# One layer of a hybrid diffusion backbone on one core: a third buffer for low parts, an own buffer for the vector product's tiles, its sums by a column of ones, and context decays made in place and earlier

## The chip, the cores and the metric

The kernel runs on one core of one Trainium2 chip. The time is the device time of one execution in microseconds (us), the median of the runs shown. The profile comes from one further execution. Its engines are named as the profile names them: PE (TensorE: matmuls; PEld is its weight load), DVE (VectorE), ACT (ScalarE), POOL (GpSimd) and SP (SyncE, which here only issues DMA transfers, in order).

## The reference

The layer has 256 latent tokens and 256 context tokens of width 2048, all in float32. Cut to what matters here:

```python
mod  = silu(c) @ w_mod + b_mod            # 6 x 2048 shifts, scales, gates; the same for the context
h    = modulate(rms_norm(x), sh1, sc1);   hc = the same for the context
q, ff, fb, v, g, a, b = split(h @ w_in)   # eight heads of 128 keys and 128 values
# per head and direction (forward with ff, backward with fb): f = lb + (1-lb)*sigmoid(ff)
#   S_t = diag(f_t) S_{t-1} + (1-f_t) v_t^T ;  o_t = S_t^T silu(q_t)
#   the latent scan starts from the final state of the context scan
y    = concat(readout(o_f + o_b, g), silu(group_norm(dwconv31(a * sigmoid(b))))) @ w_out
x    = x + g1 * rms_norm(y)
h2   = modulate(rms_norm(x), sh2, sc2)
x    = x + g2 * rms_norm((gelu(dwconv3x3(h2 @ up_gate)) * (h2 @ up_val)) @ ffn_down)
```

## The kernel before, in words

**Matmuls.** Every weight is split into a high part (`whi`, rounded to the type that PE reads at full rate) and a low part (`wlo`, the rest), and so is every activation. A product is three matmuls: high by high, high by low, low by high (`mm3_w`, `mm3_x`, lines 192 to 210). A weight tile is 128 x 2048 values, 1 MB. `wtile` (line 130) brings one: SP issues its DMA into a `raw` buffer (line 127), ACT casts it to `whi` (line 137), DVE subtracts to `wlo` (line 140). `take` hands out a tile and stages the one after it.

**Buffers.** `raw` has three buffers, `whi` three, `wlo` two. The three `raw` buffers are shared: the tiles of the modulation weights for the vector product (`graw`, line 702) use them as well. A buffer comes free when DVE has made the low part (line 140), or has added the last half of a `graw` tile (line 713).

**The vector product.** Four of the six modulation vectors (numbers s = 2 to 5) are not made on PE. For each s, 16 tiles arrive one after the other, and DVE multiplies each by its 128 values of silu(c), one per partition, and adds it to `gacc` (128 x 2048), in two halves per tile (line 713). `GEMV_H`, `GEMV_G` and `GEMV_W` say after which matrix product how many of these tiles are handed out. In the first phases their priority is lowered by `gemv_prio` = -1000. Then `gacc` has to be summed over the 128 partitions, with the result laid out as columns (`mod_cols`, line 718): in four visits PE transposes four blocks each, and ACT copies each block with an accumulated sum.

**Stages.** Phase 0 (to 158.9 us) makes the first modulation vectors, the hidden input `hT`, and v. Its tiles `mraw` are put in turn into eight free buffers of `raw`, `whi` and `wlo`. Then come eight heads: per head the products ff, fb, q (`head_gemm`), then b and a (`conv_gemm`); then eight products g. Phase 2 is the output projection and the first residual, phase 3 the wide layer up (gate and val), phase 4 the layer down.

**The attention of a head** (`head`, line 775) is spawned when its q is made, and runs under the products of the head after it. DVE and ACT first make the decays, keys and queries of seven levels in turn (lines 799 to 826, the "level chain": each level's scaling on DVE reads what ACT and DVE left of the level before). After 22 us of counted matmul time (`Y_DG`) PE comes by for the scores (line 837, tiles `lv` and `cr`). Then the diagonal blocks are picked by masks on DVE (line 850) and copied by ACT. Two scans on DVE make the context decays (lines 868 and 870) into two of the four rows of `att`, and the context keys are multiplied by them (line 873). After a further 6.5 us PE comes by for the context scores (`cx`, line 878), then for `o` (line 886), then for its transpose.

**What sets the order.** From the heads on, PE's order is the written program's (`self.order({ET.PE})`): the visits stand at fixed places between the products, and PE waits where an operand is late. DVE, ACT and SP are ordered ahead of time by a planner that goes by priority and its own durations; weight tiles are moved ahead by 600, `graw` sums put back by 1000. On the chip every engine then keeps that order, so an instruction whose operand is late holds back all that stand behind it.

Of the kernel before, what the change touches and what calls it, by code (L numbers as in the profile page):

```python
# [8 lines left out]
F32 = mybir.dt.float32  # L9
# [6 lines left out]
P = 128  # L16
# [19 lines left out]
ACT_M = 64  # L36
GEMV_H = {"ff": 2, "fb": 0, "q": 1, "b": 1, "a": 0}
GEMV_G = 0.2
# [20 lines left out]
    ("lnb", HEADS),  # L59
    ("hgw", 1),  # L60
    ("fcw", NFF * 9),
    ("fcb", NFF),
]
_POFF = {}
_n = 0
for _name, _w in _PCOLS:
    _POFF[_name] = (_n, _n + _w)
    _n += _w
NPAR = _n

# [43 lines left out]
class _Kernel:  # L114
# [15 lines left out]
    def wtile(self, i, prio=600, hi=None, lo=None):  # L130

        src, (oh, ol) = self.srcs[i], self.places[i]
        raw = self.raws.pop(0) if self.raws else self.raw_tile(src, prio)
        with self.tc.high_priority(prio):
            if hi is None:
                hi = self.stg.tile([P, WBUF], F32R, tag="whi", name="whi", bufs=3)[:, oh:oh + 2048]
            self.nc.scalar.copy(hi, raw)  # L137
            if lo is None:
                lo = self.stg.tile([P, WBUF], F32R, tag="wlo", name="wlo", bufs=2)[:, ol:ol + 2048]
            self.nc.vector.tensor_sub(lo, raw, hi.bitcast(F32))  # L140
        return hi, lo
# [81 lines left out]
    def par(self, name, i=0, n=1):  # L223
        o = _POFF[name][0]
        return self.params[:, o + i:o + i + n]

# [14 lines left out]
    def run(self):  # L241
# [44 lines left out]
        self.pax = px  # L286
        self.gemv_prio = -1000
        self.order(P0_ENG)
# [44 lines left out]
        self.hid_lo = hid.tile([P, NFF, SEQ], F32R, name="hid_lo")  # L333
        upp, up = enter(name="up", bufs=2, side="right")
        self.phase3(up)
        leave(upp)
# [12 lines left out]
    def consts(self):  # L349
# [47 lines left out]
        self.ab = cst.tile([P, 2, KB, 2], F32, name="ab")  # L397
        self.mc = cst.tile([P, 4, KB], F32, name="mc")

    def late_consts(self):  # L400
# [10 lines left out]
    def phase0(self, p0, px, srcs):  # L411
# [49 lines left out]
        def gemv_row(q, t):  # L461

            if t == 0:
                rows[q] = px.tile([P, 512], F32, tag="row", name="row", bufs=P0_ROW)
            tag, n = (("raw", 3), ("whi", 3), ("wlo", 2), ("raw", 3), ("whi", 3), ("wlo", 2), ("raw", 3), ("whi", 3))[self.nt % 8]
            self.nt += 1
            w = self.stg.tile([P, 2048 if tag == "raw" else WBUF], F32, tag=tag, name="mraw", bufs=n)[:, 0:2048]
            nc.sync.dma_start(w, a["wm1"][q, t])
# [306 lines left out]
    def head(self, h, st):  # L775
# [23 lines left out]
        for m in LEVELS:  # L799
# [16 lines left out]
            else:  # L816
                ts = T[:, :, toff:toff + nb]
                for i, o in enumerate(range(0, SEQ, 2 * m)):
                    e0, e1 = slice(o, o + m), slice(o + m, o + 2 * m)
                    for t, d, e, f in ((Q, 0, e0, ts[:, 0, 2 * i + 1:2 * i + 2]), (Q, 1, e1, ts[:, 1, 2 * i:2 * i + 1]),  # L820
# [37 lines left out]
        for j in range(4):  # L858
            r = slice(32 * j, 32 * (j + 1))
            nc.scalar.copy(_ap(att[r], 32 * j, [[SEQ + P, 2], [1, 32]]), diag[r])  # L860
# [7 lines left out]
        nc.vector.tensor_tensor_scan(_ap(E, SEQ - 2, [[-1, n]]), _ap(FF, 512 + 512 - 1, [[-1, n]]),  # L868
                                     _ap(FF, 512 + 512 - 1, [[-1, n]]), 1.0, op0=ALU.mult, op1=ALU.bypass)
        nc.vector.tensor_tensor_scan(E[:, 1, 1:SEQ], FF[:, 0, SEQ:SEQ + n], FF[:, 0, SEQ:SEQ + n], 1.0,  # L870
                                     op0=ALU.mult, op1=ALU.bypass)
        kc = KK[:, :, SEQ:512]
        nc.vector.tensor_mul(kc, kc, E)
        yield Y_CX
# [355 lines left out]
def _pack(inputs):  # L1230
# [27 lines left out]
    }  # L1258
    a["params"] = np.ascontiguousarray(np.concatenate([parts[n] for n, _ in _PCOLS], axis=1))
    i = np.arange(P)  # L1260
# [18 lines left out]
```

## Time and profile before

| | |
|---|---|
| three runs | 1419.16, 1422.34, 1422.53 us; median 1422.34 |
| profiled execution, its own time | 1419.87 us |
| its span, first to last instruction | 1418.1 us |
| mean granted PE clock | 0.995 |
| PE busy | 97% of the span |
| DVE busy | 76% |
| ACT busy | 51% |
| DMA queue of SP | 62.7% of 16 engines |

Busy times of matmuls are modelled and overlap each other, so a stage with PE at 100% has matmuls in an unbroken row; an idle time shown ahead of a matmul is a lower bound of what was lost there. "idle before <- X" names who ended a wait. Times inside the span count from its first instruction.

### The profile page before, as it was taken

The numbers are of one execution on the slowest core, as the hardware profiler recorded it, in microseconds if no ns is written. First come the engines' busy times: TensorE is split into PE (matmuls) and PEld (weight loads), VectorE is DVE, ScalarE is ACT, GpSimd is POOL, SyncE is SP. The second block draws the span as 40 slices with busy tenths as digits, with TensorE's granted clock in tenths as the row PEclk, the third lists the DMA queues.
The fourth block names the chain that finished last, engine by engine and source line by source line (L and its number), as shares of the span: only waits on it lengthen the run. The fifth ranks groups of instructions, "written<-read, shape, count | busy, mean of one in ns | idle before, by whom it ended". The sixth has DMA issues, their size and how long they took to land.

```text
span 1418.1 us, 24793 instructions
## 1 busy us (share of the span) xinstructions
PE 1375.5 (97%) x10272; PEld 1224.9 (86%) x10272; DVE 1073.3 (76%) x1577; ACT 716.6 (51%) x1174; POOL 31.2 (2%) x57
## 2 busy tenths in 40 slices
PE   4999999999999999999999999999999999999997
PEld 2566888888888898988999999999999998888886
DVE  4444788999999899777788788778878886767544
ACT  4333456666656665536744444454545443333532
POOL 0000001001000011000000000000000000000000
PEclk9999999999999999999999999999999999999999
DMA  9988676446645565788355555555555558878652
GB/s 374 391 325 330 258 267 218 160 188 238 222 167 207 208 226 189 286 305 302 123 205 180 205 185 203 181 206 189 199 184 203 193 194 340 312 287 306 242 187 106
DMA packets 49153, 329.38 MB, mean 232 GB/s; under 512 B 5392, under 2 KB 5648, under 8 KB 10896
## 3 DMA queue, kind: packets, MB, share of 16 engines
q1 hardware_dynamic: 49040, 327.80, 62.7%
q8 instruction: 80, 1.31, 0.4%
q14 instruction: 33, 0.27, 0.1%
HBM read 323.58 MB, written 4.19 MB: 231 GB/s over the span
## 4 chain that ended last, share of the span: by engine, by line
PE 77%; DVE 11%; ACT 4%; DMA 3%; issue 2%; POOL 2%; SPq 0%; DVEq 0%; POOLq 0%; ACTq 0%
PE val L197 6%; PE val L199 6%; PE val L198 6%; PE dn L206 6%; PE gate L197 6%; PE dn L208 6%; PE gate L199 5%; PE dn L207 5%; PE gate L198 5%; DVE wlo L140 3%; DVE acc L930 3%; PE v L206 2%; PE wo L208 2%; PE wo L206 2%; PE wo L207 2%
## 5 line engine op out<-in xcount | busy, mean ns | idle before, releaser
L137 ACT CAST whi<-raw 128x2048 fp32r<-128x2048 f32 x193 | 368.9, 1912 | 371.3 <-PE val L198 120.1
L140 DVE TENSOR_TENSOR wlo<-raw,whi 128x2048 fp32r<-128x2048 f32 x193 | 441.9, 2289 | 149.4 <-PE dn L207 59.7
L199 PE MATMUL val<-h,wlo 128*128 128x256 f32 x704 | 194.3, 276 | 0.0
L197 PE MATMUL val<-h,whi 128*128 128x256 f32 x704 | 194.3, 276 | 0.0
L198 PE MATMUL val<-h,whi 128*128 128x256 f32 x704 | 194.3, 276 | 0.0
L197 PE MATMUL gate<-h,whi 128*128 128x256 f32 x688 | 189.9, 276 | 0.0
L198 PE MATMUL gate<-h,whi 128*128 128x256 f32 x688 | 189.9, 276 | 0.0
L199 PE MATMUL gate<-h,wlo 128*128 128x256 f32 x688 | 189.9, 276 | 0.0
L1139 DVE SCALAR_TENSOR_TENSOR gacc<-gate,params,gacc 128x189 f32<-128x189 f32 (+2 forms) x352 | 152.4, 433 | 23.3 <-ACT gacc L1133 12.5
L206 PE MATMUL dn<-whi,hid_hi 128*128 128x512 f32 x352 | 137.4, 390 | 0.0
L208 PE MATMUL dn<-whi,hid_lo 128*128 128x512 f32 x352 | 137.0, 389 | 0.0
L207 PE MATMUL dn<-wlo,hid_hi 128*128 128x512 f32 x352 | 136.9, 389 | 0.0
L197 PEld LDWEIGHTS val<-h,whi 128*128 128x128 f32 x704 | 132.2, 188 | 0.0
L198 PEld LDWEIGHTS val<-h,whi 128*128 128x128 f32 x704 | 132.2, 188 | 0.0
L199 PEld LDWEIGHTS val<-h,wlo 128*128 128x128 f32 x704 | 132.1, 188 | 0.0
L199 PEld LDWEIGHTS gate<-h,wlo 128*128 128x128 f32 x688 | 129.2, 188 | 0.0
L197 PEld LDWEIGHTS gate<-h,whi 128*128 128x128 f32 x688 | 129.1, 188 | 0.0
L198 PEld LDWEIGHTS gate<-h,whi 128*128 128x128 f32 x688 | 129.1, 188 | 0.0
L713 DVE SCALAR_TENSOR_TENSOR big<-graw,cs,big 128x1024 f32<-128x1024 f32 x90 | 113.5, 1278 | 14.0 <-DMA graw<-in_wm_dram 13.9
L930 DVE SCALAR_TENSOR_TENSOR acc<-u,params,acc 128x242 f32<-128x242 f32 (+14 forms) x240 | 98.8, 472 | 0.0
L208 PEld LDWEIGHTS dn<-whi,hid_lo 128*128 128x128 f32 x352 | 66.1, 188 | 13.9
L207 PEld LDWEIGHTS dn<-wlo,hid_hi 128*128 128x128 f32 x352 | 66.1, 188 | 13.5
(270 smaller groups left out, 2681.4 us busy)
## 6 DMA issues: line engine op xcount, KB each, us to landing
raw<-in_wup_dram SPq DMA_DIRECT2D x88, 1024.0 KB, 4.8
graw<-in_wm_dram SPq DMA_DIRECT2D x64, 1024.0 KB, 5.0
raw<-in_win_dram SPq DMA_DIRECT2D x48, 1024.0 KB, 5.0
raw<-in_wdn_dram SPq DMA_DIRECT2D x44, 1024.0 KB, 4.9
mraw<-in_wm_dram SPq DMA_DIRECT2D x32, 1024.0 KB, 9.6
raw<-in_wout_dram SPq DMA_DIRECT2D x16, 1024.0 KB, 4.9
vraw<-in_wv_dram SPq DMA_DIRECT2D x16, 512.0 KB, 6.2
x<-in_x_dram SPq DMA_DIRECT2D x2, 1024.0 KB, 7.1
```

Of the source, the lines that this page charges most:

```text
L137: self.nc.scalar.copy(hi, raw)
L140: self.nc.vector.tensor_sub(lo, raw, hi.bitcast(F32))
L197: nc.tensor.matmul(out, wh, xh, start=start, stop=False)
L198: nc.tensor.matmul(out, wh, xl, start=False, stop=False)
L199: nc.tensor.matmul(out, wl, xh, start=False, stop=stop)
L206: nc.tensor.matmul(out, xh, wh, start=start, stop=False)
L207: nc.tensor.matmul(out, xh, wl, start=False, stop=False)
L208: nc.tensor.matmul(out, xl, wh, start=False, stop=stop)
L713: nc.vector.scalar_tensor_tensor(self.gacc[:, sl], w[:, sl], c, self.gacc[:, sl], op0=ALU.mult, op1=ALU.add)
L930: nc.vector.scalar_tensor_tensor(d, u[:, lo + o:hi + o], self.par("cw", j * CONVW + k), d, op0=ALU.mult, op1=ALU.add)
L1139: nc.vector.scalar_tensor_tensor(o, g[:, r0 + dy:r1 + dy, c0 + dx:c1 + dx], self.par("fcw", j * 9 + (dy + 1) * 3 + dx + 1), o, op0=ALU.mul ...
```

## The change

1. `wlo` gets a third buffer.
2. `graw` gets one buffer of its own and no longer uses `raw`. In phase 0, `mraw` goes round ten buffers instead of eight, the new ones among them. `GEMV_H` hands the tiles out evenly (one after each of ff, fb, q and b), and the lowered priority of their sums is gone.
3. The sums over the partitions are 16 matmuls with one column of ones as the moving operand, in one visit of PE after 12 us of counted time, into one PSUM tile; DVE adds the bias from there. PE's 16 transposes, and ACT's 16 copies with sums, go.
4. The two context scans write in place, into the decays `FF`, and with the product by the context keys they stand ahead of the 22 us visit. A two-column copy `te` keeps the two values of `T` that ACT needs after it. Two memsets of POOL per head go.
5. To make room, the parameters of the 3 x 3 convolution (440 of 921 columns) become a tile of their own, loaded before phase 3; the scratch that is set aside for another kind of DMA is cut; a pad of 56 columns is added to the constants.

```diff
-GEMV_H = {"ff": 2, "fb": 0, "q": 1, "b": 1, "a": 0}
+GEMV_H = {"ff": 1, "fb": 1, "q": 1, "b": 1, "a": 0}
...
-                lo = self.stg.tile([P, WBUF], F32R, tag="wlo", name="wlo", bufs=2)[:, ol:ol + 2048]
+                lo = self.stg.tile([P, WBUF], F32R, tag="wlo", name="wlo", bufs=3)[:, ol:ol + 2048]
...
-        self.gemv_prio = -1000
+        self.gemv_prio = 0
...
         upp, up = enter(name="up", bufs=2, side="right")
+        self.fparams = up.tile([P, NFCP], F32, name="fparams", bufs=1)
+        nc.sync.dma_start(self.fparams, a["fparams"])
         self.phase3(up)
...
+        cst.tile([P, 56], F32, name="pad")
...
-            tag, n = (("raw", 3), ("whi", 3), ("wlo", 2), ("raw", 3), ("whi", 3), ("wlo", 2), ("raw", 3), ("whi", 3))[self.nt % 8]
+            tag, n = (("raw", 3), ("whi", 3), ("wlo", 3), ("raw", 3), ("whi", 3), ("wlo", 3), ("graw", 1), ("raw", 3),
+                      ("whi", 3), ("wlo", 3))[self.nt % 10]
...
-        w = self.stg.tile([P, 2048], F32, tag="raw", name="graw", bufs=3)
+        w = self.stg.tile([P, 2048], F32, tag="graw", name="graw", bufs=1)
...
-        for q in range(4):
-            yield 2.0 if q else 5.0
-            ps = self.ax_tile("gT")
-            for j in range(4):
-                kb = q * 4 + j
-                nc.tensor.transpose(ps[:, j * P:(j + 1) * P], gacc[:, kb * P:(kb + 1) * P], self.ident)
-            for j in range(4):
-                kb = q * 4 + j
-                nc.scalar.activation(gacc[:, kb * P:(kb + 1) * P], ps[:, j * P:(j + 1) * P], AF.Copy,
-                                     accum_out=col[:, kb:kb + 1])
-        nc.vector.tensor_add(col, col, self.par("bmod", s * KB, KB))
+        yield 12.0
+        ps = self.ax_tile("gT")
+        for kb in range(KB):
+            nc.tensor.matmul(ps[:, kb:kb + 1], gacc[:, kb * P:(kb + 1) * P], self.onecol, start=True, stop=True)
+        nc.vector.tensor_add(col, ps[:, 0:KB], self.par("bmod", s * KB, KB))
...
+        te = hp.tile([P, 2], F32, tag="te", name="te")
+        nc.vector.tensor_copy(te, _ap(T, toff + 1, [[tds - 1, 2]]))
+
+        n = SEQ - 1
+        for d, o, i in ((1, 512 + 512 - 1, -1), (0, SEQ, 1)):
+            e = _ap(FF, o, [[i, n]])
+            nc.vector.tensor_tensor_scan(e, e, e, 1.0, op0=ALU.mult, op1=ALU.bypass)
+        kc = _ap(KK, SEQ, [[513, 2], [1, n]])
+        nc.vector.tensor_mul(kc, kc, _ap(FF, 512 + SEQ + 1, [[-513, 2], [1, n]]))
         yield Y_DG
...
-        nc.scalar.activation(Q[:, 0, 0:P], Q[:, 0, 0:P], AF.Copy, scale=T[:, 0, toff + 1:toff + 2])
-        nc.scalar.activation(Q[:, 1, P:SEQ], Q[:, 1, P:SEQ], AF.Copy, scale=T[:, 1, toff:toff + 1])
-
-        E = att[:, 2:4, :]
-        nc.gpsimd.memset(E[:, 0, SEQ - 1:SEQ], 1.0)
-        nc.gpsimd.memset(E[:, 1, 0:1], 1.0)
-        n = SEQ - 1
-        nc.vector.tensor_tensor_scan(_ap(E, SEQ - 2, [[-1, n]]), _ap(FF, 512 + 512 - 1, [[-1, n]]),
-                                     _ap(FF, 512 + 512 - 1, [[-1, n]]), 1.0, op0=ALU.mult, op1=ALU.bypass)
-        nc.vector.tensor_tensor_scan(E[:, 1, 1:SEQ], FF[:, 0, SEQ:SEQ + n], FF[:, 0, SEQ:SEQ + n], 1.0,
-                                     op0=ALU.mult, op1=ALU.bypass)
-        kc = KK[:, :, SEQ:512]
-        nc.vector.tensor_mul(kc, kc, E)
+        nc.scalar.activation(Q[:, 0, 0:P], Q[:, 0, 0:P], AF.Copy, scale=te[:, 0:1])
+        nc.scalar.activation(Q[:, 1, P:SEQ], Q[:, 1, P:SEQ], AF.Copy, scale=te[:, 1:2])
         yield Y_CX
...
-    nc = bacc.Bacc("TRN2", target_bir_lowering=False, num_devices=1)
+    nc = bacc.Bacc("TRN2", target_bir_lowering=False, num_devices=1, dynamic_dma_scratch_size=1024)
```

More of the change, by code (lines that the diff above doesn't have):

```diff
@@ L60 @@
     ("hgw", 1),
+]
+_FCOLS = [
     ("fcw", NFF * 9),
@@ L64 @@
 _POFF = {}
[L65 to L69, printed above, removed]
+for _list in (_PCOLS, _FCOLS):
+    _n = 0
+    for _name, _w in _list:
+        _POFF[_name] = (_n, _n + _w)
+        _n += _w
+NPAR = sum(_w for _, _w in _PCOLS)
+NFCP = sum(_w for _, _w in _FCOLS)
 def _ap(t, off, dims):
@@ L224, in par @@
         o = _POFF[name][0]
-        return self.params[:, o + i:o + i + n]
+        t = self.fparams if name in ("fcw", "fcb") else self.params
+        return t[:, o + i:o + i + n]
     def rsqrt(self, out, t):
@@ L464, in gemv_row @@
                 rows[q] = px.tile([P, 512], F32, tag="row", name="row", bufs=P0_ROW)
-            tag, n = (("raw", 3), ("whi", 3), ("wlo", 2), ("raw", 3), ("whi", 3), ("wlo", 2), ("raw", 3), ("whi", 3))[self.nt % 8]
+            tag, n = (("raw", 3), ("whi", 3), ("wlo", 3), ("raw", 3), ("whi", 3), ("wlo", 3), ("graw", 1), ("raw", 3),
+                      ("whi", 3), ("wlo", 3))[self.nt % 10]
             self.nt += 1
-            w = self.stg.tile([P, 2048 if tag == "raw" else WBUF], F32, tag=tag, name="mraw", bufs=n)[:, 0:2048]
+            w = self.stg.tile([P, WBUF if tag[0] == "w" else 2048], F32, tag=tag, name="mraw", bufs=n)[:, 0:2048]
             nc.sync.dma_start(w, a["wm1"][q, t])
@@ L1258, in _pack @@
     }
-    a["params"] = np.ascontiguousarray(np.concatenate([parts[n] for n, _ in _PCOLS], axis=1))
+    for name, cols in (("params", _PCOLS), ("fparams", _FCOLS)):
+        a[name] = np.ascontiguousarray(np.concatenate([parts[n] for n, _ in cols], axis=1))
     i = np.arange(P)
```

## The prediction

> **What bounds the kernel now.** I read the page first, then the busy time by stage, then by head, then PE's waits among the heads, and last the timeline around single waits.
>
> ```profile
> PE 1375.5 (97%) x10272; PEld 1224.9 (86%) x10272; DVE 1073.3 (76%) x1577; ACT 716.6 (51%) x1174; POOL 31.2 (2%) x57
> ...
> PE 77%; DVE 11%; ACT 4%; DMA 3%; issue 2%; POOL 2%; SPq 0%; DVEq 0%; POOLq 0%; ACTq 0%
> ```
>
> PE is busy for 97% of the span, so only 1418.1 - 1375.5 = 42.6 us of idle time can be seen at all. The stages say where it lies (columns: length, then busy time and count of PE, PEld, DVE, ACT, POOL, then clock, DMA share, GB/s):
>
> ```profile
> 0.00:18.30 18.30, 5.08 (x27) 0.79 (x27) 3.79 (x17) 5.60 (x10) 1.35 (x8) 1.00 0.90 345
> ...
> 198.72:527.79 329.07, 321.89 (x2933) 284.51 (x2931) 302.68 (x590) 211.50 (x498) 20.19 (x35) 1.00 0.55 202
> ...
> 688.26:1163.50 475.24, 475.24 (x4191) 474.97 (x4191) 379.88 (x525) 233.13 (x268) 0.00 (x0) 1.00 0.54 191
> ```
>
> Phase 3 (688 to 1163 us) has PE full: more buffers can give nothing there. The first 18.3 us are the first transfers. What this change can move is the stretch of heads, where PE and DVE (302.68 of 329.07, 92%) are both nearly full. By head, each from its ff to the next ff:
>
> ```profile
> 198.72:244.12 45.40, 45.26 (x417) 40.07 (x415) 41.56 (x82) 27.67 (x60) 3.94 (x5) 1.00 0.58 211
> 244.12:293.42 49.30, 47.28 (x433) 41.85 (x432) 44.78 (x90) 34.56 (x97) 2.27 (x5) 1.00 0.49 187
> 293.42:338.98 45.56, 45.10 (x416) 39.87 (x415) 42.67 (x83) 27.86 (x61) 3.92 (x5) 1.00 0.57 212
> 338.98:387.74 48.76, 46.08 (x416) 40.25 (x415) 45.16 (x87) 31.21 (x64) 1.94 (x5) 1.00 0.58 210
> 387.74:434.37 46.63, 45.93 (x417) 40.52 (x415) 43.47 (x85) 28.69 (x61) 1.94 (x5) 1.00 0.56 204
> 434.37:482.14 47.77, 47.05 (x432) 42.00 (x431) 42.35 (x86) 32.87 (x97) 2.27 (x5) 1.00 0.50 180
> 482.14:527.79 45.65, 45.20 (x417) 39.95 (x415) 42.68 (x83) 28.64 (x62) 3.92 (x5) 1.00 0.57 215
> sum 329.07, PE 321.89 PEld 284.51 DVE 302.68 ACT 211.50 POOL 20.19; mean PE 45.98 PEld 40.64 DVE 43.24 ACT 30.21 POOL 2.88
> ```
>
> Three heads take 45.54 on average (45.40, 45.56, 45.65); the mean is 47.01. Two of the long ones (432 and 433 matmuls where the others have 416 or 417) carry the 16 transposes of the sums. PE's waits from 158.9 to 584.6 us are these (total, times, longest):
>
> ```profile
> PE ff L199 <- DVE wlo L140: 2.1, 4, 1.0
> PE o L886 <- ACT att L880: 1.6, 3, 0.8
> PE oT L906 <- ACT on L901: 1.2, 1, 1.2
> PE a L199 <- DVE wlo L140: 1.0, 2, 0.7
> ...
> PE g L199 <- DVE wlo L140: 0.7, 1, 0.7
> ...
> PE o L886 <- ACT att L860: 0.4, 1, 0.4
> ```
>
> **Step 1: raw, graw and wlo buffers.** The longest wait for a low part can be followed back in the timeline (start, length, engine, line):
>
> ```profile
> 234.52 1.28 DVE L713 SCALAR_TENSOR_TENSOR big<-graw,cs,big 128x1024 f32<-128x1024 f32 x1
> ```
>
> ```profile
> 235.83 0.33 SPq L127 DMA_DIRECT2D raw<-in_win_dram  x1
> ```
>
> ```profile
> 241.46 1.92 ACT L137 CAST whi<-raw 128x2048 fp32r<-128x2048 f32 x1 [0.76 <-DMA raw<-in_win_dram]
> ```
>
> ```profile
> 243.41 2.29 DVE L140 TENSOR_TENSOR wlo<-raw,whi 128x2048 fp32r<-128x2048 f32 x1 [0.94 <-ACT whi L137]
> ```
>
> ```profile
> 245.75 0.50 PE L199 MATMUL ff<-hT,wlo 128*128 128x512 f32 x1 [1.01 <-DVE wlo L140]
> ```
>
> The weight tile's DMA goes out only when DVE has added the last half of a vector-product tile at 235.80, which held the shared buffer. Landing, cast and subtraction then run end to end, and PE waits 1.01 us. With three buffers for weights alone that DMA goes out a tile sooner, and the landing leaves this path. The waits on `wlo` are 2.1 + 1.0 + 0.7 = 3.8 us. The third `wlo` lets DVE subtract before PE has left the buffer two tiles back; in phases 3 and 4 PE waits for neither, so nothing is gained there. In phase 0 PE waits for `mraw` four times in the whole span, all in the first 18.3 us, before any buffer is used twice, so ten buffers instead of eight gain nothing there:
>
> ```profile
> PE row L470 <- DMA mraw<-in_wm_dram: 13.2, 4, 10.7
> ```
>
> **Step 2: the context decays.** Now they stand between the score visit and the diagonal's masks:
>
> ```profile
> 357.93 0.68 DVE L868 TENSOR_TENSOR_SCAN att<-x 128x255 f32<-128x255 f32 x1
> ...
> 358.64 0.68 DVE L870 TENSOR_TENSOR_SCAN att<-x 128x255 f32<-128x255 f32 x1
> ...
> 359.42 0.69 DVE L873 TENSOR_TENSOR x<-x,att 128x512 f32<-128x512 f32 x1
> ```
>
> That is 2.05 us of DVE, moved ahead. Behind it the mask copies, ACT's copies into `att` and `o` can come up to 2.05 us sooner, and the next head's decays, which wait for the scans, too. PE's waits for `att` (1.6 + 0.4) and for `oT` (1.2) are what this can shorten, 3.2 us; I take half, since ACT's casts stand in the same queue. The score visit could be late by 2.05 us if the scans ran ahead of the level chain, but they come after it in the order. No row shows a scan whose output is its input: nearest is the same scan, 0.68 us; as the lower end I take 0.35, half of the product's 0.69 for twice the length, as the upper twice 0.68. That is -0.7 to +1.4 us of DVE per head for both scans, against 47.01 - 43.24 = 3.8 us of DVE idle: no cost. The `te` copy and the lost memsets are small work on engines with room.
>
> Both steps together should bring the heads towards the length of the three short ones. The five heads without sums take 232.00 us; 5 x 45.54 = 227.70, so -4.3. The two with sums, less 1.75 for their transposes (below), take 47.55 and 46.02; at 45.54 that is -2.5. The waits of the first head and of g add about -1.0. In all **-7.8**, from 0 (DVE sets the length) to -11.
>
> **Step 3: the sums.** Rows for the price (the first three PE in the chain and the timeline, the last two PEld with mean ns at the end):
>
> ```profile
> 224.13 1.80 PE o L886 x16
> 584.85 1.75 PE gbc L745 x16
> ```
>
> ```profile
> 212.31 0.85 PE L837 MATMUL lv<-qm,km 128*32 128x32 f32 x78
> ```
>
> ```profile
> L886 PEld LDWEIGHTS o<-v,att 128*128 128x128 f32 x128 | 15.6, 191 | 3.5 <-ACT att L880 2.2 <-ACT att L860 0.8
> ...
> L837 PEld LDWEIGHTS lv<-qm,km 128*32 128x32 f32 x640 | 6.4, 109 | 0.0
> ```
>
> A transpose is one record, 16 in 1.75 us. A float32 product is two (`o`: 64 products, 128 records), each with its own weight load. So a sweep becomes 32 records with 128 columns of weights and one moving column, a form no row shows. Upper end: 1.80/16 = 0.112 us each, 3.6 us. Lower end: the narrow scores, 0.85/78 = 0.011 for 32 columns, so 0.044 for 128 and 1.4 us. A load of 128 columns takes 191 ns, one of 32 takes 109: 0.85 ns per column, 109 ns for 128, and it can't hide behind one moving column. So I take the upper end less a little, 3.5 us: +1.75 per sweep. Four sweeps (two among the heads, one each in phases 2 and 4) make **+7.0**; with the lower end -1.4. ACT loses 16 copies per sweep, which stand beside PE's work.
>
> The Trainium skill, page "TensorE: Matmul & The Clock Gate", section "Back-to-back issue gap", gives about 81 ns for a weight load and a matmul of 128 columns in a long row. By it a sweep is 2.6 us and the whole 3.6 us less; no row here comes below 109 ns with full weights, so the trace doesn't bear it out.
>
> **Step 4: parameters and queues.**
>
> ```profile
> graw<-in_wm_dram SPq DMA_DIRECT2D x64, 1024.0 KB, 5.0
> ...
> params<-in_params_dram SPq DMA_DIRECT2D x1, 460.5 KB, 3.4
> ```
>
> 440 of 921 columns, 220 KB, leave the head of the queue; at 345 GB/s that is **-0.6** for all that follows. They come back on SP's queue ahead of phase 3, 3.4 us or less for what is needed only at the first gate, some us after 688; should they be issued last, after the store of x1, about 2 us would show, once. One `graw` buffer means 5.0 us of landing and two halves of 1.28 on DVE, 7.6 us per tile. A head of 47 us brings four, so it keeps up; the first head's seven (39.8 us) run on into the second, where nobody waits for them. A `graw` issue that waits on SP holds the weights queued behind it, but up to three tiles are then ahead, 5.4 us or more of PE each. The pad, the scratch and POOL's memsets cost nothing that the profile shows.
>
> **Sum.** -7.8 + 7.0 - 0.6 = -1.4 on the profiled execution's 1419.87: 1418.5. The median of the runs is 2.5 higher, the lowest run 0.7 lower. I say **1418**.
>
> **Rivals.**
>
> *Cheap sums.* If a weight load runs beside the one before it, as four narrow ones do in the scores, a sweep costs 1.4 us: 1418.5 - 8.4 = 1410. For it speaks the narrow row, against it every row of full weights.
>
> *No relief.* If DVE, not the landing, makes the low parts late, the heads keep their length: 1419.87 + 7.0 - 0.6 = 1426. For it: at 92% DVE has little room. Against it: the wait followed back above.
>
> *DVE waits for graw.* This one makes the kernel slower. With ordinary priority the sums stand where the planner expects the landing, and DVE, in order, stops with all behind it: level chain, masks, low parts, and so PE. The waits of the sums on a landing (total, times) are, over the whole span:
>
> ```profile
>   DVE big L713: 13.9, 9
>   DVE gacc L713: 9.4, 4
> ```
>
> That is 1.5 us each among the first nine. If each of a head's four tiles waits so, DVE needs 43.24 + 6.2 = 49.4, 2.4 above 47.01; seven heads give +17, sums outside the heads +3.5: 1440. It decides from 3.8/4 = 0.95 us per tile on; at 1.2 us it is 1.0 per head and 1430. Against it: most landings found DVE busy (13 waits in 64 tiles).
>
> **Chances.** A difference of 0.3%, 4.3 us, is about what a measurement of this kernel can tell from no change. The forecast (1412 to 1424) has 0.50, of which 0.20 is faster by more than that and 0.30 within. Cheap sums 0.22, faster. No relief 0.12, half within, half slower. DVE waits for graw 0.16, slower. So faster 0.42, within 0.36, slower 0.22. The likeliest case's own range is 1412 to 1424; the range for 8 in 10 is 1406 to 1429.
>
> **What would show it.** Right: heads without sums at 45 to 46 us, no wait of ff, a or g on `wlo`, `raw` landing well ahead of the cast, PE's 32 records of `gT` in about 3.5 us per sweep, the first `row` matmuls about 0.6 us sooner, phase 3 unchanged. Wrong: sweeps of 1.4 to 2.6 us, heads above 46.5, DVE idle ahead of line 713, a wait at the score visit, or SP held by `graw` while ACT waits for `raw`.

## The result, and the profile after

The changed kernel takes **1460.79 us** (median of four runs, 1458.62 to 1462.51) where the kernel before takes 1421.93 in the same comparison (1419.16 to 1422.53). The ratio is 1.0280, 95% interval 1.0265 to 1.0295. It is 39 us slower; the prediction said 1418, with a range up to 1429. Executions that took over 1.5% longer than the fastest of their kernel are left out of the ratios; the profiled executions of `late_decays` and `one_graw_alone` below are among them.

The profiled execution took 1458.62 us, with a span of 1456.8 and a mean granted PE clock of 0.983 (before 0.995). The page's busy times and the engines' shares of its chain:

```profile
PE 1394.1 (96%) x10336; PEld 1243.2 (85%) x10336; DVE 1068.3 (73%) x1585; ACT 702.0 (48%) x1046; POOL 25.9 (2%) x41
...
PE 76%; DVE 14%; issue 3%; DMA 3%; ACT 3%; POOL 1%; SPq 0%; POOLq 0%; DVEq 0%; ACTq 0%
```

PE has 64 more records, all of them sums, but it is busy for 18.6 us more, and idle for 62.7 instead of 42.6. DVE does less than before and yet has 14% of the chain instead of 11%. The stages say where this lies: first seven of the eight heads (each from its ff to the next ff), then phases 2 and 3 (columns as in the prediction):

```profile
198.70:254.00 55.30, 47.16 (x417) 41.21 (x415) 50.19 (x95) 29.81 (x65) 3.62 (x3) 0.94 0.62 227
254.00:306.28 52.28, 50.14 (x448) 45.15 (x447) 43.53 (x85) 27.73 (x60) 2.15 (x3) 0.97 0.56 189
306.28:354.85 48.57, 45.48 (x417) 40.30 (x415) 45.09 (x87) 28.88 (x62) 2.53 (x3) 1.00 0.58 211
354.85:401.88 47.03, 45.10 (x416) 39.90 (x415) 44.03 (x89) 29.41 (x65) 2.54 (x3) 1.00 0.57 202
401.88:448.03 46.15, 45.12 (x416) 40.03 (x415) 43.42 (x84) 28.59 (x61) 1.68 (x3) 1.00 0.61 210
448.03:502.32 54.29, 51.63 (x448) 46.31 (x447) 40.85 (x86) 28.84 (x62) 2.00 (x3) 0.94 0.45 161
502.32:552.24 49.92, 47.13 (x416) 41.49 (x415) 44.90 (x86) 28.90 (x62) 2.54 (x3) 0.97 0.55 202
...
609.18:725.38 116.20, 107.99 (x515) 91.34 (x513) 75.90 (x78) 54.64 (x77) 2.59 (x4) 0.96 0.68 253
725.38:1204.20 478.82, 478.82 (x4228) 478.82 (x4226) 377.36 (x527) 237.97 (x269) 0.00 (x0) 1.00 0.55 190
```

From the first ff to the end of g it is 449.35 us instead of 425.79 (+23.6), and phase 2 takes 116.20 instead of 103.32 (+12.9); phase 0 adds 0.9, phase 4 adds 1.8, and phase 3 loses 0.5. That is the whole 38.7 us of span. Of the 23.6 us, PE is idle for 13.2 more and busy for 10.3 more, of which 3.8 are the records of two sweeps (a sweep is one vector's sum over the partitions). The rest of the busy time goes with the clock: the same 416 or 417 matmuls take PE 45.1 to 45.5 us in the heads at a clock of 1.00 and 47.1 where it is 0.94 to 0.97. PE's waits (total, times, longest):

```profile
PE row L481 <- DMA mraw<-in_wm_dram: 13.3, 4, 10.8
PE cr L851 <- DVE x L840: 12.5, 6, 4.4
PE cT L967 <- ACT un L962: 7.1, 6, 3.0
PE x2T L92 <- issue: 6.3, 1, 6.3
PE cr L851 <- ACT Q L827: 3.5, 4, 1.0
```

No wait on `wlo` is left, where the heads and g had 3.8 us. In its place PE waits at the score visit (`cr`) for the product that the moved decays end in, and at `cT` (0.7 us before the change) for the norm behind the convolution. The timeline of the worst score visit, under the second head's products, shows how (start, length, engine):

```profile
211.88 0.85 PE L851 MATMUL lv<-qm,km 128*32 128x32 f32 x78
...
212.36 2.28 DVE L145 TENSOR_TENSOR wlo<-raw,whi 128x2048 fp32r<-128x2048 f32 x1
...
213.88 0.42 PE L851 MATMUL cr<-Q,x 128*32 128x128 f32 x8 [0.76 <-ACT Q L827]
...
214.56 2.47 DVE L724 SCALAR_TENSOR_TENSOR big<-graw,cs,big 128x1024 f32<-128x1024 f32 x2
...
216.96 0.68 DVE L838 TENSOR_TENSOR_SCAN x<-x 128x255 f32<-128x255 f32 x1
...
217.93 0.68 DVE L840 TENSOR_TENSOR x<-x 128x510 f32<-128x510 f32 x1
...
218.66 0.65 PE L851 MATMUL cr<-Q,x 128*32 128x128 f32 x8 [4.35 <-DVE x L840]
...
219.25 0.80 PE L202 MATMUL fb<-hT,whi 128*128 128x512 f32 x1
...
219.84 0.63 PE L203 MATMUL fb<-hT,whi 128*128 128x512 f32 x1
```

PE's scores of the levels run at 211.88, so PE was there, and the first eight records of `cr` ran at 213.88. The other eight waited for the product (line 840). On DVE a low part (2.28 us) and the sums of a vector-product tile (2.47 us) stood ahead of the second scan. `cr` doesn't read the context keys that the product makes, only the latent ones. But the product is one access over both directions, from column 256 of the first to the end of the second, and the second direction's latent keys lie in between; the run `split_keys` below shows that the wait hangs on this. PE lost 4.35 us, and then more: the matmuls behind it show 0.63 us instead of 0.39. The windows around it (the column after POOL's is the granted clock):

```profile
205.00:212.00 7.00, 7.00 (x63) 5.56 (x62) 6.74 (x19) 3.47 (x7) 0.00 (x0) 1.00 0.71 261
212.00:218.60 6.60, 1.55 (x129) 1.12 (x115) 6.60 (x9) 2.81 (x12) 0.00 (x0) 0.80 0.49 182
218.60:222.40 3.80, 3.74 (x15) 2.69 (x16) 3.80 (x13) 2.50 (x6) 0.00 (x0) 0.50 0.71 293
222.40:230.00 7.60, 7.60 (x34) 6.36 (x33) 7.03 (x17) 2.39 (x9) 0.00 (x0) 0.97 0.42 140
```

After the wait the clock stood at 0.50 for 3.8 us, which is 1.9 us of full clock lost: this wait was paid about one and a half times (6.2 us for 4.35, an estimate from these rows). The Trainium skill, page "TensorE: Matmul & The Clock Gate", section "Part 1: The HAM clock gate (the "warmup" mystery)", says that the clock falls to half after an idle window of about 3.4 us and comes back after as long a busy one; these rows agree, with 0.50 for 3.8 us behind a pause of 4.35 and 0.97 over the 7.6 us after that.

Phase 2 has one long wait as well. The last tile of the third vector is summed late. The timeline of the kernel before, then that of the changed kernel, then a window of it:

```profile
643.66 2.47 DVE L713 SCALAR_TENSOR_TENSOR big<-graw,cs,big 128x1024 f32<-128x1024 f32 x2
```

```profile
685.65 2.48 DVE L724 SCALAR_TENSOR_TENSOR big<-graw,cs,big 128x1024 f32<-128x1024 f32 x2 [1.90 <-DMA graw<-in_wm_dram]
...
705.43 3.76 PE L92 MATMUL x2T<-dg,x 128*128 128x128 f32 x16 [6.34 <-issue]
```

```profile
700.00:710.00 10.00, 4.57 (x19) 4.41 (x20) 4.51 (x9) 3.66 (x8) 0.56 (x1) 0.71 0.57 211
```

DVE waited for its landing, and the sums are done 42 us later than before (688.13 against 646.13); phase 2 itself begins 24.5 us later, so within it they are 17.5 us late. PE stood idle for 6.34 us ahead of the transposes after the first residual, with a clock of 0.71 over 700 to 710. These transposes don't read the third vector; they wait for the residual of the first token block. In the kernel before, 36 matmuls of the second block run under that residual. In the changed kernel's timeline 21 of them have run earlier, around the late sums, and 15 are left. With two buffers (`two_graw` below) the last tile is summed by 617.65, all 36 run under the residual again, and the wait is gone. Why a late tile puts those 21 ahead is not followed further.

### The profile page after: what moved, and what is told of

Its sections match the earlier page's. It is cut to its first block, busy times and chain, and to the rows that moved or that the text cites. A ratio compares the mean times of both kernels' runs of the same rounds, so it can differ in the third digit from the quotient of the medians.

```text
span 1456.8 us, 24793 instructions
## 1 busy us (share of the span) xinstructions
PE 1394.1 (96%) x10336; PEld 1243.2 (85%) x10336; DVE 1068.3 (73%) x1585; ACT 702.0 (48%) x1046; POOL 25.9 (2%) x41
## 4 chain that ended last, share of the span: by engine, by line
PE 76%; DVE 14%; issue 3%; DMA 3%; ACT 3%; POOL 1%; SPq 0%; POOLq 0%; DVEq 0%; ACTq 0%
PE val L204 5%; PE val L202 5%; PE val L203 5%; PE dn L211 5%; PE dn L212 5%; PE gate L204 5%; PE gate L202 5%; PE dn L213 5%; PE gate L203 5%; DVE wlo L145 4%; DVE big L724 3%; DVE acc L933 2%; DMA graw<-in_wm_dram 2%; PE v L211 2%; PE wo L211 2%
## 5 line engine op out<-in xcount | busy, mean ns | idle before, releaser
L1142 DVE SCALAR_TENSOR_TENSOR gacc<-gate,fparams,gacc 128x189 f32<-128x189 f32 (+2 forms) x352 | 152.1, 432 | 10.9
L933 DVE SCALAR_TENSOR_TENSOR acc<-u,params,acc 128x241 f32<-128x241 f32 (+14 forms) x240 | 103.8, 470 | 0.0
L213 PEld LDWEIGHTS dn<-whi,hid_lo 128*128 128x128 f32 x352 | 66.1, 188 | 13.8
L211 PEld LDWEIGHTS dn<-whi,hid_hi 128*128 128x128 f32 x352 | 66.1, 188 | 13.7
```

The source lines that it names most:

```text
L211: nc.tensor.matmul(out, xh, wh, start=start, stop=False)
L213: nc.tensor.matmul(out, xl, wh, start=False, stop=stop)
L933: nc.vector.scalar_tensor_tensor(d, u[:, lo + o:hi + o], self.par("cw", j * CONVW + k), d, op0=ALU.mult, op1=ALU.add)
L1142: nc.vector.scalar_tensor_tensor(o, g[:, r0 + dy:r1 + dy, c0 + dx:c1 + dx], self.par("fcw", j * 9 + (dy + 1) * 3 + dx + 1), o, op0=ALU.mul ...
```

## The experiments

Each kernel was timed beside the kernel before on the same chip; differences in us below are the ratio less 1, times 1421.

**First, four edits to the changed kernel, one at a time.** The two readings at this point: that the moved decays were badly made (one product over both directions, which makes `cr` wait though it doesn't read the result), or that DVE as a whole was late at the visit.

```diff
-        kc = _ap(KK, SEQ, [[513, 2], [1, n]])
-        nc.vector.tensor_mul(kc, kc, _ap(FF, 512 + SEQ + 1, [[-513, 2], [1, n]]))
+        for k, f in ((SEQ, 512 + SEQ + 1), (512 + SEQ + 1, SEQ)):
+            kc = _ap(KK, k, [[1, n]])
+            nc.vector.tensor_mul(kc, kc, _ap(FF, f, [[1, n]]))
```

> The changed kernel with one edit: the product of the context keys by the decays is written as two products, one per direction, each over its own 255 columns, instead of one whose access jumps from one direction's half to the other's. Theory A (the score visit is made to wait for a product that it does not read): in the changed kernel PE waits 12.5 us in six waits of cr on that product, because its one access spans from column 256 of the first direction to the end of the second, over the latent keys of the second direction that cr reads. With two accesses nothing is shared: these waits go, and the time falls by 10 to 14 us, to about 1447 to 1451. Rival B (DVE is simply late, because the vector product's sums stand ahead of everything): cr then waits for what else is late on DVE, and the time falls by less than 4 us, or rises a little for the 8 extra instructions (8 x about 0.1 us).

Measured: ratio 1.0354 (1.0252 to 1.0456), no better than the change. PE's waits:

```profile
PE cr L852 <- ACT att L811: 7.6, 3, 3.4
...
PE o L890 <- ACT att L875: 6.2, 5, 3.1
```

The same visit as above, on PE and on DVE:

```profile
213.58 0.89 PE L852 MATMUL cr<-Q,x 128*32 128x128 f32 x16 [0.51 <-ACT Q L827]
```

```profile
217.53 0.42 DVE L841 TENSOR_TENSOR x<-x 128x255 f32<-128x255 f32 x1
```

All 16 records of `cr` now run 4 us ahead of the second product: the scores never needed it, and the wait came from the one access. The waits for the product (12.5 us) are gone, but others took their place, at this visit in other heads and at `o`, where ACT's copies are late. So how the product is made causes the wait at `cr`, but not the loss.

The decays put back behind the visit, as before the change (`te` goes with them):

```diff
-        te = hp.tile([P, 2], F32, tag="te", name="te")
...
-            nc.vector.tensor_tensor_scan(e, e, e, 1.0, op0=ALU.mult, op1=ALU.bypass)
...
         yield Y_DG
...
+        nc.vector.tensor_tensor_scan(_ap(E, SEQ - 2, [[-1, n]]), _ap(FF, 512 + 512 - 1, [[-1, n]]),
...
         yield Y_CX
```

> The changed kernel with step 4 undone: the two scans, their product with the context keys and the two memsets are behind the score visit again, in att, as before. Theory A: the 12.5 us of waits on the product go, as with two products, and the scans no longer run ahead of it; the old waits of the next head's decays on the scans come back but cost PE little (o on att 2 us, oT 1 us). Expected 1446 to 1452. Rival B (sums ahead on DVE): the 2.05 us of DVE per head come back between visit and masks, where vector-product sums stand already, so o is later than before the change: 1456 to 1464.

Measured: 1.0171 (1.0088 to 1.0254), +24 us, give or take 12. In the changed kernel the early decays thus cost some 15 us, with the same uncertainty, but 24 remain without them.

The sums of the vector product put back by 1000 again:

```diff
-        self.gemv_prio = 0
+        self.gemv_prio = -1000
```

> The changed kernel with the sums of the vector product put back by 1000 again in phase 0 and the heads. Theory B (sums at ordinary priority stand ahead of level chain, masks and norm on DVE, 2.5 us a tile): the waits of cT on un (7.1 us), of cr on the level chain's scaling (3.5 us) and part of cr's on the product (12.5 us) go: 1440 to 1448. Rival A: only the norm's waits go, about 1452. Rival D (one buffer): a put-back sum holds the only buffer, up to the 20 us seen before the change, so that the vector product falls further behind, the sums of the last vector come later still in phase 2, where PE already loses 12.9 us against before, and the time stays at 1458 or rises to 1470.

Measured: 1.0697 (1.0613 to 1.0781), +99 us. PE's longest wait:

```profile
PE gT L736 <- DVE big L724: 69.1, 3, 36.5
```

With one buffer, sums that are put back hold up the next tile's transfer, tile after tile, until PE stands waiting for the vector. So the ordinary priority came with the one buffer: the put-back sums don't go with it.

The sums over the partitions as before the change, by transposes in four visits:

```diff
-        yield 12.0
-        ps = self.ax_tile("gT")
-        for kb in range(KB):
-            nc.tensor.matmul(ps[:, kb:kb + 1], gacc[:, kb * P:(kb + 1) * P], self.onecol, start=True, stop=True)
+        for q in range(4):
+            yield 2.0 if q else 5.0
...
+                nc.tensor.transpose(ps[:, j * P:(j + 1) * P], gacc[:, kb * P:(kb + 1) * P], self.ident)
```

> The changed kernel with the sums over the partitions as before: 16 transposes in four visits and 16 copies with sums on ACT. By the trace of the changed kernel a sweep of 32 records takes 3.63 us against about 1.75 for the transposes: four sweeps give 7.5 us back, so 1453 if PE's time alone counts. If ACT's 16 copies per sweep (about 4.4 us) were in the way, as the change supposes, less comes back: 1456 to 1460. If the visit after 12 us in one piece is what makes the last vector late in phase 2, more: 1445.

Measured: 1.0373 (1.0283 to 1.0464). PE waits 14.9 us for the vector product at the transposes, since their first visit comes early and the vector comes late. The changed kernel has no such wait; that its one late visit is what keeps it out is argued from this.

**Second, the buffer count against the priority, and two parts alone.** The changed kernel with two buffers for `graw`; the room comes from the third low part:

```diff
-        w = self.stg.tile([P, 2048], F32, tag="graw", name="graw", bufs=1)
+        w = self.stg.tile([P, 2048], F32, tag="graw", name="graw", bufs=2)
...
-                lo = self.stg.tile([P, WBUF], F32R, tag="wlo", name="wlo", bufs=3)[:, ol:ol + 2048]
+                lo = self.stg.tile([P, WBUF], F32R, tag="wlo", name="wlo", bufs=2)[:, ol:ol + 2048]
```

> The changed kernel with two buffers for the vector product's tiles instead of one, and two for the low parts instead of three (the room is the same); everything else, the ordinary priority too, as in the changed kernel. If the one buffer is the root (its cycle of issue, 5.0 us of landing and 2.5 us on DVE makes the product late), the last tile of the third vector is summed near 646 us as before the change and not at 688, phase 2 falls from 116.2 to near 104 us plus 3.7 for two sweeps' difference, and the whole is 1440 or less. If the ordinary priority is the root (2.5 us of sums stand ahead of the level chain and the masks), the heads keep some 50 us on average and the whole stays at 1450 or more even with phase 2 mended.

Measured: 1.0135 (1.0108 to 1.0163), +19 us: this takes back half of the loss. Phase 2 is 108.3 us, and its wait of 6.3 us is gone. The third low part went with the same edit; alone it gives no gain (`third_low_alone` below).

The same with the lowered priority as well:

```diff
-        self.gemv_prio = 0
+        self.gemv_prio = -1000
```

> As the run with two buffers, but with the vector product's sums put back behind all other work of DVE, as in the kernel before the change. With one buffer the put-back sums took 1522 us (heads of 91 and 82 us, in which PE waited for the vector). If the cycle of one buffer was the reason, two buffers bring this down to the forecast of 1418 to 1426: heads at 46 to 48 us and phase 2 near 105. If instead a buffer of its own makes put-back sums wait longer whatever their number, because no weight tile needs the room any more and nothing pulls them forward, heads 2 and 6 stay above 55 us and the whole stays above 1450.

Measured: 1.0133 (1.0110 to 1.0156). The priority, which with one buffer stood for ratios of 1.0280 and 1.0697, makes no difference that can be measured with two. So half of the loss hangs on the one buffer, and the ordinary priority is its consequence. But 19 us are still there.

The new sums alone, in the kernel before:

```diff
-        for q in range(4):
-            yield 2.0 if q else 5.0
...
+        yield 12.0
...
+            nc.tensor.matmul(ps[:, kb:kb + 1], gacc[:, kb * P:(kb + 1) * P], self.onecol, start=True, stop=True)
```

> The kernel before the change, with the sums by a column of ones alone: 32 records instead of 16 transposes, one visit with a due time of 12 instead of four. The trace of the changed kernel gives 3.63 us for a sweep among the heads and 4.79 in phase 2 against 1.75. If only that price counts, it is 4 x 1.9 = 7.5 us slower: 1427 to 1430. If the one late visit also makes the vector's columns late for those who need them, PE waits for them and it is over 1432; if the 16 copies that leave ACT gain more than the records cost, it is 1424 or less.

Measured: 1.0076 (1.0057 to 1.0095), +10.8 us, more than the records' price. The trace shows what else is paid (timeline of PE, then windows):

```profile
466.59 4.79 PE L725 MATMUL gT<-onecol,big 128*128 128x1 f32 x32
471.24 0.56 PE L197 MATMUL q<-hT,whi 128*128 128x256 f32 x1
471.60 0.41 PE L198 MATMUL q<-hT,whi 128*128 128x256 f32 x1
```

```profile
466.50:471.40 4.90, 4.90 (x36) 4.90 (x35) 0.81 (x4) 2.56 (x5) 0.87 (x1) 0.74 0.67 216
471.40:475.00 3.60, 3.60 (x17) 3.60 (x18) 3.01 (x10) 1.14 (x3) 1.38 (x2) 0.50 0.01 2
```

PE isn't idle here, and yet the clock fell in the sweep and stood at 0.50 for 3.6 us behind it. It did so in two of the four sweeps. In the changed kernel, too, the 3.6 us behind the two sweeps among the heads were at 0.68 and 0.77.

The early decays in place alone, in the kernel before:

```diff
+            nc.vector.tensor_tensor_scan(e, e, e, 1.0, op0=ALU.mult, op1=ALU.bypass)
...
         yield Y_DG
...
-        nc.vector.tensor_tensor_scan(E[:, 1, 1:SEQ], FF[:, 0, SEQ:SEQ + n], FF[:, 0, SEQ:SEQ + n], 1.0,
```

> The kernel before the change, with the context decays in place and ahead of the score visit alone. If they cost nothing there (the forecast's step 2), it is 1418 to 1421 us and PE does not wait for the scores' operands. If the score visit has no 2 us to spare (the last operand of the level chain is ready 0.3 to 2.6 us before the visit in the kernel before), PE waits at the visit by 0.5 to 2 us per head and the whole is 1424 to 1436. If the product's store into the keys is what the visit waits for only when the sums stand ahead of it, it lies between, at 1420 to 1424.

Measured: 1.0021 (1.0010 to 1.0032), +3.0 us. PE now waits a little at the score visit, and at `o` for 4.2 us where it had 1.6:

```profile
PE o L884 <- ACT att L878: 4.2, 4, 1.5
...
PE cr L846 <- DVE x L835: 1.3, 2, 0.7
```

**Third, the buffers alone, in four forms.** Sums and decays are as before the change, parameters as in it. The first is an edit to the changed kernel and keeps its own form: one buffer for `graw`, three low parts, ordinary priority, and the tiles handed out evenly (`GEMV_H`).

```diff
-        yield 12.0
+        for q in range(4):
...
-            nc.vector.tensor_tensor_scan(e, e, e, 1.0, op0=ALU.mult, op1=ALU.bypass)
```

> The changed kernel with the old sums (transposes, four visits) and the context decays back behind the score visit. What is left is step 1 in the form of the change: one buffer of its own for the vector product's tiles at ordinary priority, three low-part buffers, plus step 4. If the one buffer with its ordinary priority is what cost the time, this alone is 1440 to 1455 us, the heads take 49 us or more on average and phase 2 is 112 us or longer, because the last vector is late. If the loss comes from the sums and the early decays (10.8 and 3.0 us when each is put into the kernel before), this is 1412 to 1424, as the forecast had it for step 1 (-7.8 and -0.6).

Measured: 1.0305 (1.0255 to 1.0354), +43 us. The change's form of the buffers alone costs as much as the whole change. The even handing out is part of this form; no run tries it by itself.

The other three are edits to the kernel before, so the sums are put back by 1000 and the tiles handed out as they were. Two buffers of their own and two for the low parts:

```diff
-        w = self.stg.tile([P, 2048], F32, tag="raw", name="graw", bufs=3)
+        w = self.stg.tile([P, 2048], F32, tag="graw", name="graw", bufs=2)
```

> The kernel before with two buffers of their own for the vector product's tiles (sums behind all other work of DVE, as before), three for the weights alone, two for the low parts, and step 4; sums and decays as before. The forecast's step 1 in its intended form: raw buffers no longer wait for the vector product. If the landing behind a shared buffer is what makes the low parts late, PE's waits for the low parts (3.8 us) go, and the heads without sums come down to 45.5 us: 1412 to 1417. If it was only where the wait was booked, and DVE (92% busy) or the order sets the heads, it is 1419 to 1424. If put-back sums in a buffer of their own run too late for their vectors, the heads with sums grow and it is over 1426.

Measured: 1.0018 (0.9996 to 1.0040), +2.6 us, no difference that can be told. With the new sums and early decays beside it (10.8 and 3.0) that makes 16.4, near the 18.9 of `two_graw_low`, so most of what two buffers left is these two parts. Here the low parts are relieved as the forecast had it: no wait on `wlo` is left. PE's only long wait among the heads is another, which was 0.7 us before the change:

```profile
PE cT L974 <- ACT un L969: 13.8, 7, 5.2
```

Four buffers shared by weights and vector product, two for the low parts:

```diff
-            raw = self.stg.tile([P, 2048], F32, tag="raw", name="raw", bufs=3)
+            raw = self.stg.tile([P, 2048], F32, tag="raw", name="raw", bufs=4)
...
-        w = self.stg.tile([P, 2048], F32, tag="raw", name="graw", bufs=3)
+        w = self.stg.tile([P, 2048], F32, tag="raw", name="graw", bufs=4)
```

> The kernel before with a fourth shared buffer for weights and vector-product tiles (the room of one tile, as in the change), and step 4. The buffers stay common, so a vector tile that waits for DVE holds one of four instead of one of three, and a weight tile that needs the room pulls its sum forward. If the landing behind a held buffer is the loss of the kernel before, this gains most of the 3.8 us and part of the heads' excess over 45.5: 1410 to 1417. If nothing is to be had from buffers, 1419 to 1423.

Measured: **1416.84 us** (1415.56 to 1418.89, twelve runs), ratio 0.9962 (0.9940 to 0.9984), -5.4 us: 0.4% faster than the kernel before. From the first ff to the end of g it takes 421.53 us instead of 425.79; the waits on `wlo` are 2.0 us and the wait at `cT` is 5.8. A difference between the shared form and the own form shows in DVE's work on `graw` in that stretch (start and end, length, busy time). The kernel before, two of its own, four shared:

```profile
158.90:584.69 425.79, 92.44 (x75) 1.00 0.59 215
```

```profile
160.84:589.43 428.59, 106.52 (x86) 0.98 0.60 223
```

```profile
162.06:583.59 421.53, 91.68 (x75) 1.00 0.59 217
```

With two buffers of their own, 14 us more of the sums fall among the heads, where DVE is 92% busy before the change, instead of in phase 2, where it is busy for 74.59 of 103.32 us. With four shared buffers it is as much as before the change. That this extra work makes the longer wait at `cT` is argued, not tried by itself. What makes up the gain of the shared form, beyond the 1.8 us less of waits on `wlo`, stays open.

Three shared as before the change, and a third for the low parts alone:

```diff
-                lo = self.stg.tile([P, WBUF], F32R, tag="wlo", name="wlo", bufs=2)[:, ol:ol + 2048]
+                lo = self.stg.tile([P, WBUF], F32R, tag="wlo", name="wlo", bufs=3)[:, ol:ol + 2048]
```

> The kernel before with the third buffer for low parts alone (shared weight buffers stay three) and step 4. If the waits on low parts come from DVE, which cannot subtract before PE has left the buffer two tiles back, they go and it is 1414 to 1418. If they come from the landing, as the forecast's step 1 followed them back, the waits on low parts stay at 3 us or more and the time stays at 1419 to 1422.

Measured: 1.0027 (0.9995 to 1.0060): no gain that can be told. The forecast gave this buffer no price of its own.

**Last, the two questions left.** The sums by ones in four visits, in the kernel before:

```diff
         for q in range(4):
             yield 2.0 if q else 5.0
...
+                nc.tensor.matmul(ps[:, j:j + 1], gacc[:, kb * P:(kb + 1) * P], self.onecol, start=True, stop=True)
+            nc.vector.tensor_add(col[:, q * 4:q * 4 + 4], ps[:, 0:4], self.par("bmod", s * KB + q * 4, 4))
```

> The kernel before with the sums by a column of ones, but in four visits of eight records (due times 5, 2, 2, 2, as the transposes had) instead of one visit of 32. The one visit alone cost 10.8 us where its records are worth 4 x 1.9 = 7.5; after two of its four sweeps the granted clock stood at 0.50 for some 3.5 us and the same matmuls took nearly twice as long. If a long row of records with one moving column is what lets the clock down, eight records (0.9 us) at a time do not: no stretch at 0.50 behind the sums, heads and phase 2 longer than before by 1.9 us per sweep, 1427 to 1429 in all. If the clock falls for another reason, or the 10.8 us come from the lateness of the one visit, it stays at 1430 or more, or falls to 1424 with the sums of the records unchanged.

Measured: 1.0057 (1.0020 to 1.0093); by time it can't be told from the one visit. The profiled execution took 1445.62 us because its phase 3, which has no sweep, took 497.91 instead of 479.27, so only stages ahead of it are compared. Phase 2 with one visit, then with four:

```profile
589.41:697.65 108.24, 106.62 (x515) 89.94 (x513) 74.22 (x75) 54.04 (x75) 2.59 (x4) 0.97 0.71 267
```

```profile
588.04:693.25 105.21, 103.59 (x514) 87.38 (x513) 74.87 (x78) 54.13 (x75) 2.59 (x4) 1.00 0.74 275
```

The same records take 3.0 us less in four visits, at a clock of 1.00: 1.9 above the 103.32 of before, which is the records' own price. The two heads with sums are at 1.00 as well (1.00 and 0.93 with one visit) and take 97.5 us instead of 101.4. So it is the long row of one-column records that lets the clock down; how much of the 10.8 us it makes in all stays open, since these are single executions.

The whole change, with four shared buffers, two low parts, the lowered priority and the handing out of before in place of its own form of the buffers:

```diff
-GEMV_H = {"ff": 1, "fb": 1, "q": 1, "b": 1, "a": 0}
+GEMV_H = {"ff": 2, "fb": 0, "q": 1, "b": 1, "a": 0}
...
-        self.gemv_prio = 0
+        self.gemv_prio = -1000
...
-        w = self.stg.tile([P, 2048], F32, tag="graw", name="graw", bufs=1)
+        w = self.stg.tile([P, 2048], F32, tag="raw", name="graw", bufs=4)
```

> The whole change with the buffers alone in another form: four shared buffers for weights and the vector product's tiles, two for the low parts, and the sums put back behind DVE's other work, instead of three, one of its own and three at ordinary priority. New sums, early decays in place, parameters as in the change. If the form of the buffers is what the 39 us hang on, the parts add up: four shared buffers alone -5.4, sums 10.8, decays 3.0, so 1421 + 8.4 = 1427 to 1433. If the early decays or the sums are what makes the change slow whatever the buffers, it stays above 1438.

Measured: 1428.37 us, 1.0058 (1.0042 to 1.0074), +8.2 us, where the parts add up to -5.4 + 10.8 + 3.0 = +8.4. With the buffers in this form the parts add up. In the change's form they don't: the buffers alone cost 43 us, with the new sums beside them 24, and with the early decays too 39.

## Why the prediction was wrong, step by step

The step that failed worst is step 4's "so it keeps up", with the one buffer it speaks of: the prediction put this buffer and the ordinary priority that goes with it at nothing. The change's form of the buffers alone cost 43 us, two buffers of their own +2.6 and four shared ones -5.4. The gain of steps 1 and 2 didn't come either.

**Steps 1 and 2, -7.8.** From the first ff to the end of g the change took +23.6; less two sweeps at 1.9 that is +19.8 instead of -7.8.

- The wait that was followed back is real, and it goes: no wait on `wlo` is left. Wrong was the sentence that both steps "should bring the heads towards the length of the three short ones". What the long heads have above 45.5 us was not only that wait: in `two_graw_alone`, where the low parts are relieved, PE waits 13.8 us at `cT` instead of 0.7. The rival *No relief* had the time right for buffers of their own: +2.6 us there, not apart from 0. Only with shared buffers did a gain come, 5.4 us, within the forecast's 0 to 11, and 2.0 us of waits on `wlo` are left there.
- "They come after it in the order" was right of the scans and missed the point. With the product written as one access over both directions the visit waits for it, though the scores don't read it, and ahead of it DVE does whatever the planner put there, 4.75 us in the visit shown. With the product in two halves that wait goes and the time doesn't: ACT's copies are late at `cr` and `o` instead, and why is not followed further. Step 2 was to gain 1.6 us; alone it cost 3.0, and with one buffer about 15. The price of a scan in place was right: 0.68 us.

**Step 4 failed at "so it keeps up".** 7.6 us per tile against four tiles in a head counted landing and sums end to end, but not the wait for DVE's turn; the third vector ended 42 us later than before, 17.5 us later within phase 2. Phase 2 took +12.9, of which 1.9 are a sweep's records and 6.6 more idle time of PE. And the one buffer made the ordinary priority needed (+99 us without it), which the prediction treated as a rival's detail and not as a cost of step 4. This is SP's wait among the heads and g (total, times, longest):

```profile
SPq L714 <- DVE big L724: 82.0, 23, 6.0
```

SP held the next tile's issue in 23 cases until DVE had summed the last one: the cycle runs through DVE's queue, which the 7.6 us left out. The -0.6 for the parameters isn't to be seen: PE's wait for the first tiles is 13.3 us where it was 13.2, and phase 0 is no shorter.

**Step 3, +7.0, was right in its mechanism and short in size.** A sweep takes 3.63 us (3.5 were said):

```profile
286.22 3.63 PE L736 MATMUL gT<-onecol,big 128*128 128x1 f32 x32
```

Four sweeps at 3.63 instead of 1.75 would be 7.5 us; alone the sums cost 10.8. What the trace shows beyond the records is the granted clock in and behind a sweep, which the prediction doesn't have. The rival *Cheap sums* is out.

**The rival on the slower side** named the right place and the wrong mechanism. *DVE waits for graw* meant DVE standing idle ahead of the sums; among the heads and g that is 10.3 us in 7 waits, on DVE:

```profile
DVE big L724 <- DMA graw<-in_wm_dram: 10.3, 7, 5.5
```

In the visit shown, the sums themselves ran ahead of what PE waited for, 2.47 us of them, next to a low part of 2.28; that this is the larger part over the whole stretch is argued from this. Its 1430 to 1440 was too little as well: it priced no lower clock, and PE's busy time is 18.6 us longer, 7.5 of them the sums' records.

Of the signs named for being wrong, heads above 46.5 us (six of the seven), a wait at the score visit and SP held by `graw` came. Of those named for being right, the waits on `wlo` went and phase 3 stayed the same.

## What to carry to other kernels

A transfer's cycle in a buffer runs through the queue of the engine that empties it: with one buffer, count the wait for that engine's turn, and ask what priority the work must then have and whom it will stand in front of. When the engine that frees a buffer is nearly full, relieving one wait need not gain its length: here another took its place. One shared buffer more was worth more here than two of their own. And what is put ahead of a visit of PE can make that visit wait for everything that stands in front of it; check that an access which spans more than it writes doesn't tie the visit to it. The wait of 4.35 us cost PE about one and a half times its length.

## What was not expected of the hardware

A pause of PE of 4.35 us was followed by 3.8 us at a granted clock of 0.50. A row of 32 records with 128 columns of weights and one moving column, in which PE shows no idle time, was in two of four cases followed by 3.6 us at 0.50 as well, and itself took 4.79 and 4.24 us instead of 3.63; in rows of eight, 0.95 us each, the clock was 1.00 in phase 2 and in both heads with sums. A scan whose output is its input took 0.68 us, as one that writes elsewhere.
